# A hybrid recurrent decoder layer on one core: two more Strassen pairs, four fewer filler blocks, and four smaller edits

## The chip, the cores and the metric

The kernel runs on one core of a Trainium2 chip. The metric is the time of one execution on the device, in microseconds (us). A core has five engines with queues of their own: PE (matrix products), DVE (vector), ACT (activation functions, and copies out of the accumulators), POOL (a second, slower vector engine) and SP, which here issues the DMA transfers. PEld is PE's loading of weights. Each engine takes its instructions in the order in which they were written into its queue, and waits on semaphores for the others.

## The reference

One step of a one-layer decoder: 16 meta tokens and 1024 prompt tokens (1040 in one sequence), and 8 samples of 4 tokens; 1072 tokens in all, width 1024, in float32. What comes out for the meta tokens is dropped from the output; their effect on the recurrent states stays.

```
xn = rmsnorm(h) * norm_w
(gq, gk, gv, glr, gg, hq, hf, hi, hg_g, mq, mk, mv, mi, mf, mo, mg, ca, cb, cg, mgate) = split(xn @ w_in)
A (GLA):    S_t = diag(exp g_t) S_{t-1} + k_t^T v_t ; o_t = q_t S_t,     zA = head_rmsnorm(o) * silu(gg)
B (HGRN2):  the same recurrence with f from hf, k = 1 - f, q = silu(hq), zB = head_rmsnorm(o) * silu(hg_g)
C (mLSTM):  stabilised matrix memory,                                    zC = head_layernorm(h * sigmoid(mo)) * silu(mg)
D (conv):   u = ca * sigmoid(cb); yc = causal depthwise conv of width 31, zD = silu(layernorm(yc)) * silu(cg)
mixed = sum_b sigmoid(mgate_b) * (z_b @ w_branch_b)        # four gates of 1024 columns: 32 blocks of 128
y = rmsnorm(h + mixed @ w_out) * final_norm                # and the final states of A, B, C and D
```

## The kernel before

All projections take x transposed, 128 rows by 1072 tokens for each of 8 row blocks. To keep float32 accuracy, each operand is split into a high and a low part (`xh`, `xl` for x; `wh`, `wl` for weights, by `split_w`: ACT makes the high part, POOL or DVE subtracts to get the low one, L138 and L139), and each product is three matmuls: high by high, high by low, low by high (L185 to L187, or L277 to L279).

The program has five stages.

- **Front** (L147 to L181): nine row tiles `h` of x are loaded, normalised (squares on ACT L164, scaling on DVE L167) and transposed by PE in three groups (L174); ACT and DVE then write `xh` (L178) and `xl` (L179) out of the accumulators, of which five are used for this. Beside that, the first gate block's weights `w0` are loaded and split, the split's second half on DVE. `gate_direct(j)` projects one gate block of 128 columns directly: three groups of 352 tokens (the meta tokens are skipped), each of 8 row blocks and 3 products, and writes the sigmoid to memory (`gscr`). Blocks 0 to 3 are done this way, with the small projections between.
- **Pairs**: `pair` computes two blocks of 128 columns at once by Strassen's scheme: x is halved by rows (4 and 4 row blocks) and by tokens (536 and 536), and 7 products replace 8. Each product is done for two halves of 268 tokens, so a pair is 7 x 2 x 4 x 3 = 168 matmuls. Sums of weights are made on DVE (`ta`, `tb`) and split there; sums of results are made on DVE out of the accumulators. Accumulators of tag "a" (`sa`) number two, those of tag "r" (`sb`, `sc`, `sd`) five, in rotation. c11 is what takes the first result out of `sa`, c12, c22 and c21 take the others. `pair_to` uses a pair for gates, for `cg` and for the output gates of the branches, 15 in all; `conv_pair` uses four for `cb` and `ca`. Its results go into a tile `u`, of which there is one; the 31 taps of the convolution are then 31 operations on DVE over 1024 tokens (L386 and L388), which the scheduler puts between the other work at a lower priority.
- **Mixers**: four HGRN units (`hg_unit`), two GLA units for two heads each (`gla_unit`), four mLSTM units. An HGRN or GLA unit goes through seven levels of block sizes 1 to 64 (`levels`): small products `lv` on PE, then DVE scales q and k (L649 to L652) for the next level. In between stand projections of the next unit, and **fillers**: `filler()` takes the next gate block of a list and projects it directly. `linear_unit` calls it `3 - nh` times, which is twice in an HGRN unit (nh = 1) and once in a GLA unit (nh = 2); an mLSTM unit calls it once, the last three times: 16 in all. Of 32 gate blocks 4 are direct in front, 10 in pairs, 2 late and 16 fillers.
- **Branches and output**: the four branch products, gated and added, then the output projection and the final norm.

In a GLA unit the diagonal of the attention is summed apart: `prod` (q times k) is multiplied with two columns of ones (L760), with 128 rows of `prod` at a time as weights. `split3` (L557, accumulator `v9p`) splits the samples' values; its accumulator comes from the pool of projections (three buffers, tag "acc").

The order on each engine is made by a scheduler from its own estimate of durations and from priorities; a change of one piece rearranges the rest.

Of the kernel before, what the change touches and what calls it, by code (L numbers as in the profile page):

```python
# [16 lines left out]
AF = mybir.ActivationFunctionType  # L17
ALU = mybir.AluOpType
# [9 lines left out]
P = 128  # L28
# [37 lines left out]
def trunk(ctx, tc, hx, w_in, w_sm, w_br, w_out, pk, wgk2, mlb, fnorm, s_gla, s_hg, s_c, s_n, s_m, s_cv,  # L66
# [80 lines left out]
    xh = xp.tile([P, KD, NT], F32R, name="xh", tag="xh")  # L147
    xl = xp.tile([P, KD, NT], F32R, name="xl", tag="xl")
    with tc.tile_pool(name="x0", bufs=9, side="right", reuse_waits="tile") as x0:
        hs = []  # L150

        def load_h(i):
            n = min(P, NT - i * P)
            h = x0.tile([P, D], F32, name="h", tag="h")
            DMA.dma_start(h[:n], hx[i * P:i * P + n, :])
            hs.append((h, n))

        for i0 in (0, 3, 6):
            for i in range(i0, i0 + 3):
                load_h(i)  # L160
                h, n = hs[i]
                ss = x0.tile([P, 1], F32, name="ss", tag="ss", bufs=9)
                sq = x0.tile([P, D], F32, name="sq", tag="sq", bufs=1)
                S.activation(sq[:n], h[:n], AF.Square, accum_out=ss[:n])  # L164
                V.tensor_scalar(ss[:n], ss[:n], 1.0 / D, EPS, ALU.mult, ALU.add)
                rs = rsqrt(ss[:n])
                V.tensor_scalar(h[:n], h[:n], rs, None, ALU.mult)  # L167
            if i0 == 0:
                raw0 = load_raw(w_in, OFF["gate"])
            for k in range(KD):  # L170
                ps = mmt("xt")
                t = 0
                for h, n in hs[i0:i0 + 3]:
                    T.transpose(ps[:, t:t + n], h[:n, k * P:(k + 1) * P], ident[:n, :n])  # L174
                    t += n
                nw = col("norm_w", k)
                hi = xh[:, k, i0 * P:i0 * P + t]
                S.activation(hi, ps[:, :t], AF.Identity, scale=nw)  # L178
                V.scalar_tensor_tensor(xl[:, k, i0 * P:i0 * P + t], ps[:, :t], nw, hi, ALU.mult, ALU.subtract)  # L179
            if i0 == 0:  # L180
                w0 = split_w(raw0, E=V)  # L181

    def mm3(ps, wh, wl, ah, al, kd, order=None):
        for i, k in enumerate(order or range(kd)):
# [20 lines left out]
    def gtl(tag, shape, bufs=1, name=None, dt=F32):  # L205
        return pools["gph"].tile(shape, dt, name=name or tag, tag=tag, bufs=bufs)
# [42 lines left out]
        xs.update(a11=a(0, 0), a12=a(KH, 0), a22=a(KH, HT), s1=a(0, HT), s2=(sh[:, 0], sl[:, 0]),  # L249
                  s3=(sh[:, 1], sl[:, 1]), s4=(sh[:, 2], sl[:, 2]))  # L250

    def pair(c0, c1, c11, c12, c22, c21):


        wp = pools["gph"]
# [14 lines left out]
        ps = lambda tag: [pools["ps"].tile([P, 512], F32, name="s" + tag, tag="a" if tag == "a" else "r",  # L270
                                           bufs=2 if tag == "a" else 5)[:, :HS] for _ in range(2)]

        def prod(w, o, x, s, out, start, stop):
            xa, xb = (t[:, :, s * HS:(s + 1) * HS] for t in xs[x])
            for k in range(KH):
                wh, wl = w[0][:, o + k], w[1][:, o + k]
                T.matmul(out, wh, xa[:, k], start=start and k == 0, stop=False, skip_group_check=True)  # L277
                T.matmul(out, wh, xb[:, k], start=False, stop=False, skip_group_check=True)  # L278
                T.matmul(out, wl, xa[:, k], start=False, stop=stop and k == KH - 1, skip_group_check=True)  # L279
# [12 lines left out]
            prod(w2, 0, "s1", s, c[s], True, True)  # L292
            S.activation(h(p5, s), c[s], AF.Copy)
        for s in range(2):
            prod(w1, KH, "a12", s, a[s], False, True)
            c11(s, a[s])
        d = ps("d")
        for s in range(2):
# [3 lines left out]
        V.tensor_tensor(u3, u3, u2, ALU.add)  # L302
        c22(u3)
        for s in range(2):
            prod(w4, 0, "s4", s, c[s], False, True)
            V.tensor_tensor(h(p1, s), h(u2, s), c[s], ALU.add)
        c12(p1)
        for s in range(2):
# [4 lines left out]
    def pair_to(sec, i, dst, func, times=False, base=0):  # L313
# [24 lines left out]
                    DMA.dma_start(dst[j, :, 0:HT - NM], t[:, NM:])  # L338
            return ev

        pair(o, o + P, c11, rest(i + 1, False), rest(i + 1, True), rest(i, True))

    def conv_pair(i):
        u = gtl("u", [P, UW + NSEQ * 34])
        us = u[:, UW:].rearrange("p (s x) -> p s x", x=34)
        G.memset(u[:, 0:30], 0.0)

        def c11(s, ps):
            S.activation(u[:, 30 + s * HS:30 + (s + 1) * HS], ps, AF.Sigmoid)  # L349

        def c12(t):
            V.tensor_tensor(u[:, 30:30 + HT], t, u[:, 30:30 + HT], ALU.mult)

        held = []

        def c21(t):
            S.activation(t, t, AF.Sigmoid)
            m = NP - HT
            V.tensor_tensor(u[:, 30 + HT:UW], held[0][:, :m], t[:, :m], ALU.mult)
            x3 = lambda v: v[:, m:].rearrange("p (s j) -> p s j", j=NDEC)  # L360
            V.tensor_tensor(us[:, :, 30:34], x3(held[0]), x3(t), ALU.mult)

        pair(OFF["cb"] + i * P, OFF["ca"] + i * P, c11, c12, held.append, c21)
        return u, us
# [73 lines left out]
                DMA.dma_start(fscr[p, :, t0:t0 + n], gx)  # L438

    open_pool("gph", bufs=1)  # L440
    gate_direct(0, w=w0)
    gate_direct(1)
    small()
    for j in range(2, NDIR):
        gate_direct(j)
# [2 lines left out]
    open_pool("ps", bufs=2, space=PSUM)  # L448
    open_pool("pm", bufs=1, space=PSUM)
    LATE = (8, 9)  # L450
    NFILL = 16
    fill = list(range(32 - NFILL, 32))
    todo = [("gate", i, gscr, AF.Sigmoid) for i in range(NDIR, 32 - NFILL, 2) if i not in LATE]
    todo += [("cg", i, cscr, AF.Copy) for i in (0, 2)]
# [120 lines left out]
    def vtok(sec, i, ones_col=False):  # L575
# [9 lines left out]
        proj(sec, i, GA, ev)  # L585
        vt = tl("vt", [P, 9, 129], 4)
        (to_tok_v(vf, vt) if ones_col else to_tok(vf, vt, True))
        v9 = split3(x9, 1, "v9", 4, acc_tile("v9p"))
        if ones_col:
            G.memset(vt[:, :, 128:129], 1.0)  # L590
        return vt, v9
# [162 lines left out]
    def linear_unit(uid, qv, nh, k, f, prod, vts, s0, epss, finish, pout, sout):  # L754
        rw = P // nh
        if nh == 2:
            ps = mmt("dg")
            for c in range(9):
                n = csz(c)
                T.matmul(ps[:n, 2 * c:2 * c + 2], prod[:, c * P:c * P + n], onesb, start=True, stop=True)  # L760
            dg = tl("dg", [P, 18], 2)
            V.tensor_copy(dg[:, 0:16], ps[:, 0:16])
            V.tensor_copy(dg[:TAIL, 16:18], ps[:TAIL, 16:18])
            dgv = dg.rearrange("p (c a) -> p c a", a=2)
        atts, tot128, tot16, tot4 = levels(qv, nh, k, f)
        for _ in range(3 - nh):
            filler()
        kt = tl("kt", [P, 9, P], 1)
        to_tok(k, kt)
        xk = tl("xk", [P, 3, NT - NP], 1)  # L770
# [576 lines left out]
```

## Time and profile before

| | us |
|---|---|
| median of 3 runs (1597.06 to 1597.72) | 1597.33 |
| the profiled execution | 1597.18 |
| its span, first to last instruction | 1595.4 |
| PE busy (its matmuls' ends are modelled) | 1558.2 |
| DVE busy | 1035.6 |
| ACT busy | 554.0 |
| POOL busy | 470.9 |

Times in the profile count from the start of the span. A stage is placed by its lines: the front ends near 45 us, the pairs run from about 95 to 510, the mixers from there to about 1270 (the last level of the last GLA unit begins near 1001), and branches and output to the end. PEclk is the share of its full clock that PE was granted. A row of the waits names who waited for whom, then us in total, times and the longest. A row of a timeline has its start, its duration, the engine, the line and operation, and in brackets the idle time before it and what ended it.

### The profile page before, as it was taken

What the parts mean: (1) busy time and instruction counts of PE and PEld (TensorE: products, weight loads), DVE (VectorE), ACT (ScalarE), POOL (GpSimd) and SP (SyncE); (2) the same over time, 40 slices, a digit from 0 to 9 for tenths busy, and PEclk for the clock granted to TensorE, in tenths of its full rate; (3) what the DMA queues carried; (4) which work ended last, traced back from release to release, by engine and by line L of the source; (5) the groups of instructions that cost most, each with busy time, mean ns of one, the idle gap of its engine ahead of it and who ended that gap; (6) DMA issues with size and microseconds to landing.
All of it is one profiled execution on the core that took longest, in us unless ns stands there. A gap on an engine that the chain in (4) does not pass through costs nothing.

```text
span 1595.4 us, 30033 instructions
## 1 busy us (share of the span) xinstructions
PE 1558.2 (98%) x12366; PEld 1496.5 (94%) x12366; DVE 1035.6 (65%) x1827; ACT 554.0 (35%) x1095; POOL 470.9 (30%) x418
## 2 busy tenths in 40 slices
PE   7999999899999999999999999999999999999998
PEld 6999999899999899999998998999999999999886
DVE  7959979999996446444544565476665646744533
ACT  6534343243433333323424323323323244422211
POOL 2222322123223232223232323222322313877300
PEclk9999999999999999999999999999999999999999
DMA  5423233231337113131323132144323277676231
GB/s 190 133 80 101 92 91 107 88 108 51 110 100 236 42 48 104 56 100 56 104 60 94 55 97 82 49 148 135 117 72 88 89 248 224 179 236 208 80 111 54
DMA packets 190572, 176.40 MB, mean 111 GB/s; under 512 B 9260, under 2 KB 164800, under 8 KB 190436
## 3 DMA queue, kind: packets, MB, share of 16 engines
q1 hardware_dynamic: 190436, 174.49, 35.6%
q8 instruction: 97, 1.59, 0.4%
q14 instruction: 39, 0.32, 0.1%
HBM read 122.45 MB, written 52.00 MB: 109 GB/s over the span
## 4 chain that ended last, share of the span: by engine, by line
PE 78%; DVE 16%; issue 3%; DMA 2%; ACT 1%; SPq 0%; DVEq 0%; POOLq 0%; ACTq 0%
PE acc L187 18%; PE acc L185 18%; PE acc L186 18%; DVE y L388 7%; PE lv L636 2%; DVE wl L139 2%; PE sa L277 1%; PE sa L278 1%; PE sa L279 1%; PE sc L278 1%; PE sc L277 1%; PE sc L279 1%; PE sd L279 1%; PE op L800 1%; PE sd L278 1%
## 5 line engine op out<-in xcount | busy, mean ns | idle before, releaser
L139 POOL TENSOR_TENSOR wl<-wraw,wh 128x1024 fp32r<-128x1024 f32 (+1 forms) x124 | 272.2, 2196 | 632.7 <-ACT wh L138 628.0
L185 PE MATMUL acc<-xh,wh 128*128 128x352 f32 (+2 forms) x1320 | 437.5, 332 | 2.1 <-ACT vt L539 1.2
L187 PE MATMUL acc<-xh,wl 128*128 128x352 f32 (+2 forms) x1320 | 436.7, 331 | 0.0
L186 PE MATMUL acc<-xl,wh 128*128 128x352 f32 (+2 forms) x1320 | 435.5, 330 | 0.0
L185 PEld LDWEIGHTS acc<-xh,wh 128*128 128x128 f32 x1320 | 251.7, 191 | 5.6 <-ACT vt L539 1.9
L187 PEld LDWEIGHTS acc<-xh,wl 128*128 128x128 f32 x1320 | 251.0, 190 | 3.2 <-issue 0.9
L186 PEld LDWEIGHTS acc<-xl,wh 128*128 128x128 f32 x1320 | 251.4, 190 | 1.8 <-issue 0.7
L388 DVE SCALAR_TENSOR_TENSOR y<-u,pkt,y 128x1024 f32<-128x1024 f32 x120 | 191.2, 1593 | 0.7
L138 ACT ACTIVATE wh<-wraw 128x512 fp32r<-128x512 f32 (+1 forms) x125 | 110.4, 883 | 231.0 <-PE acc L186 135.8
L185 PE MATMUL acc<-zh,wh 128*128 128x352 f32 x384 | 124.5, 324 | 0.0
L186 PE MATMUL acc<-zl,wh 128*128 128x352 f32 x384 | 124.3, 324 | 0.0
L187 PE MATMUL acc<-zh,wl 128*128 128x352 f32 x384 | 124.2, 324 | 0.0
L277 PE MATMUL sa<-xh,wh 128*128 128x268 f32 x304 | 88.7, 292 | 6.6 <-ACT u L349 6.3
L278 PE MATMUL sa<-xl,wh 128*128 128x268 f32 x304 | 88.2, 290 | 0.0
L279 PE MATMUL sa<-xh,wl 128*128 128x268 f32 x304 | 87.8, 290 | 0.0
L651 DVE TENSOR_TENSOR q<-q,tot 128x256 f32<-128x256 f32 (+3 forms) x96 | 46.4, 483 | 54.5 <-PE lv L636 53.7
L1179 POOL TENSOR_TENSOR mix<-mix,gt 128x352 f32<-128x352 f32 x72 | 73.1, 1030 | 28.9 <-DVE gt L1178 25.7
L185 PEld LDWEIGHTS acc<-zh,wh 128*128 128x128 f32 x384 | 72.2, 188 | 0.4 <-DVE gt L1178 0.4
L187 PEld LDWEIGHTS acc<-zh,wl 128*128 128x128 f32 x384 | 72.3, 188 | 0.0
L186 PEld LDWEIGHTS acc<-zl,wh 128*128 128x128 f32 x384 | 72.2, 188 | 0.0
L277 PEld LDWEIGHTS sa<-xh,wh 128*128 128x128 f32 x304 | 58.3, 192 | 7.3 <-ACT u L349 6.8
L1178 DVE TENSOR_TENSOR gt<-acc,gt 128x352 f32<-128x352 f32 x72 | 36.2, 518 | 39.5 <-PE acc L187 36.6
(393 smaller groups left out, 3367.3 us busy)
## 6 DMA issues: line engine op xcount, KB each, us to landing
wraw<-w_in SPq DMA_DIRECT2D x92, 512.0 KB, 3.9
gt<-gscr SPq DMA_DIRECT2D x30, 528.0 KB, 4.7
gscr<-gd SPq DMA_DIRECT2D x60, 176.0 KB, 1.8
zr<-zscr SPq DMA_DIRECT2D x16, 528.0 KB
wraw<-w_br SPq DMA_DIRECT2D x32, 256.0 KB, 2.9
gt<-sscr SPq DMA_DIRECT2D x12, 528.0 KB, 4.1
zscr<-gt SPq DMA_DIRECT2D x12, 528.0 KB, 2.6
sscr<-u SPq DMA_DIRECT2D x16, 268.0 KB, 2.3
```

What stands on the lines that cost most here:

```text
L138: S.activation(hi[:, :kd], raw[:, :kd], AF.Copy)
L139: (E or G).tensor_tensor(lo[:, :kd], raw[:, :kd], hi[:, :kd], ALU.subtract)
L185: T.matmul(ps, wh(k), ah(k), start=(i == 0), stop=False)
L186: T.matmul(ps, wh(k), al(k), start=False, stop=False)
L187: T.matmul(ps, wl(k), ah(k), start=False, stop=(i == kd - 1))
L277: T.matmul(out, wh, xa[:, k], start=start and k == 0, stop=False, skip_group_check=True)
L278: T.matmul(out, wh, xb[:, k], start=False, stop=False, skip_group_check=True)
L279: T.matmul(out, wl, xa[:, k], start=False, stop=stop and k == KH - 1, skip_group_check=True)
L388: V.scalar_tensor_tensor(ymain, u[:, NM + j:NM + j + NPR], w(j), ymain, ALU.mult, ALU.add)
L651: V.tensor_tensor(qx[:, :, 1], qx[:, :, 1], pv[r, :, 0:1].broadcast_to([rw, nb, h]), ALU.mult)
L1178: V.tensor_tensor(gt[:, t0:t0 + n], ps[:, :n], gt[:, t0:t0 + n], ALU.mult)
L1179: G.tensor_tensor(mixed[j][:, t0:t0 + n], mixed[j][:, t0:t0 + n], gt[:, t0:t0 + n], ALU.add)
```

## The change

- `NFILL` goes from 16 to 12: four gate blocks move from the mixers into two more pairs, at the end of the gates in the list of pairs. `linear_unit` calls one filler whatever nh.
- `prod` in `pair` gets `m`: in `pair_to`, the products a12 and s4 leave out the first 16 tokens (the meta tokens, which nobody reads there) of their first half.
- `conv_pair` writes its sigmoid into a buffer `g11` of its own (the pairs' own tag, two buffers), not into `u`.
- The diagonal sums are made in bands of 32 rows of weights.
- In front, the weights of gate blocks 0 and 1 are both loaded before the later rows of x, and both split with DVE.
- `v9p` takes its accumulator from the general pool (three buffers, tag "mm").

Lines after the convolution's pair move by four, in the units by six: L352 becomes L356, L388 becomes L392, L649 and L651 become L653 and L655, L760 becomes L766.

```diff
-                raw0 = load_raw(w_in, OFF["gate"])
+                raws = [load_raw(w_in, OFF["gate"] + j * P) for j in range(2)]
             for k in range(KD):
...
-            if i0 == 0:
-                w0 = split_w(raw0, E=V)
+                if i0 == 0 and k in (1, 5):
+                    wg01.append(split_w(raws[k // 4], E=V))
...
-    def pair(c0, c1, c11, c12, c22, c21):
+    def pair(c0, c1, c11, c12, c22, c21, m=0):
...
-        def prod(w, o, x, s, out, start, stop):
-            xa, xb = (t[:, :, s * HS:(s + 1) * HS] for t in xs[x])
+        def prod(w, o, x, s, out, start, stop, m=0):
+            m = m if s == 0 else 0
+            out = out[:, m:]
+            xa, xb = (t[:, :, s * HS + m:(s + 1) * HS] for t in xs[x])
...
-            prod(w1, KH, "a12", s, a[s], False, True)
+            prod(w1, KH, "a12", s, a[s], False, True, m)
...
-            prod(w4, 0, "s4", s, c[s], False, True)
+            prod(w4, 0, "s4", s, c[s], False, True, m)
...
-        pair(o, o + P, c11, rest(i + 1, False), rest(i + 1, True), rest(i, True))
+        pair(o, o + P, c11, rest(i + 1, False), rest(i + 1, True), rest(i, True), NM)
...
         u = gtl("u", [P, UW + NSEQ * 34])
+        g11 = stt("g11")
...
-            S.activation(u[:, 30 + s * HS:30 + (s + 1) * HS], ps, AF.Sigmoid)
+            S.activation(g11[:, s * HS:(s + 1) * HS], ps, AF.Sigmoid)
...
-            V.tensor_tensor(u[:, 30:30 + HT], t, u[:, 30:30 + HT], ALU.mult)
+            V.tensor_tensor(u[:, 30:30 + HT], t, g11, ALU.mult)
...
-    gate_direct(0, w=w0)
-    gate_direct(1)
+    for j in range(2):
+        gate_direct(j, w=wg01[j])
...
-    NFILL = 16
+    NFILL = 12
...
-        v9 = split3(x9, 1, "v9", 4, acc_tile("v9p"))
+        v9 = split3(x9, 1, "v9", 4, mmt("v9p"))
...
-                T.matmul(ps[:n, 2 * c:2 * c + 2], prod[:, c * P:c * P + n], onesb, start=True, stop=True)
+                for b in range(0, n, 32):
+                    e = min(b + 32, n)
+                    T.matmul(ps[b:e, 2 * c:2 * c + 2], prod[:, c * P + b:c * P + e], onesb, start=True, stop=True,
+                             skip_group_check=True)
...
-        for _ in range(3 - nh):
-            filler()
+        filler()
```

How the instructions move shows at three places. The first is ACT's order in an HGRN unit, from the unit's values (`vt`) over its levels (`att`) to the level's end (`kt`); `gd` is a filler's eviction, `f` the next unit's forget gate. Before:

```order
L560 ACTIVATE v_7680<-v9p 96x128
L217 ACTIVATE gd<-acc 128x352 x2
L138 ACTIVATE wh<-wraw 128x1024
L217 ACTIVATE gd<-acc 128x352
L688 ACTIVATE att_5615<-own 32x8x32 x4
L217 ACTIVATE gd<-acc 128x352
L676 ACTIVATE att_5615<-lv 32x4x32 x4
L217 ACTIVATE gd<-acc 128x352
L676 ACTIVATE att_5615<-lv 64x4x64 x2
L138 ACTIVATE wh<-wraw 128x1024
L217 ACTIVATE gd<-acc 128x352
L539 ACTIVATE kt<-tt 128x512 x2
```

and with the change:

```order
L217 ACTIVATE gd<-acc 128x352 x2
L138 ACTIVATE wh<-wraw 128x1024
L217 ACTIVATE gd<-acc 128x352
L692 ACTIVATE att_6079<-own 32x8x32 x4
L879 ACTIVATE f<-acc 128x358
L880 ACTIVATE k<-acc 128x358
L680 ACTIVATE att_6079<-lv 32x4x32 x4
L879 ACTIVATE f<-acc 128x358
L880 ACTIVATE k<-acc 128x358
L680 ACTIVATE att_6079<-lv 64x4x64 x2
L138 ACTIVATE wh<-wraw 128x1024
L879 ACTIVATE f<-acc 128x356
```

Where the second filler stood, the next unit's projection hf stands now; before, it came after the levels.

The second place is DVE's order at the third convolution pair, with the last taps into `y`, and `u`, `p`, `sc` of this pair and the next. Before:

```order
L267 TENSOR_TENSOR tb<-wraw,ta 128x512
L139 TENSOR_TENSOR wl<-ta,wh 128x1024
L388 SCALAR_TENSOR_TENSOR y<-u,pkt,y 128x1024 x2
L359 TENSOR_TENSOR u<-u_2958,u_2904 128x504
L361 TENSOR_TENSOR u<-u_2958,u_2904 128x8x4
L352 TENSOR_TENSOR u<-p_2903,u 128x536
```

and with the change:

```order
L139 TENSOR_TENSOR wl<-ta,wh 128x1024
L392 SCALAR_TENSOR_TENSOR y<-u,pkt,y 128x1024
L356 TENSOR_TENSOR u<-p_2909,g_2875 128x536
L363 TENSOR_TENSOR u<-u_2964,u_2910 128x504
L365 TENSOR_TENSOR u<-u_2964,u_2910 128x8x4
L304 TENSOR_TENSOR u_3191<-u_3191,p_3190 128x536
```

The multiplication into `u` stays behind the last tap; its second operand is now `g`.

The third is ACT's order in front, where the first group's `xh` ends and the second's begins. Before:

```order
L178 ACTIVATE xh<-xt,pkt 128x384
L164 ACTIVATE sq,ss<-h 128x1024
L138 ACTIVATE wh<-wraw 128x1024
L164 ACTIVATE sq,ss<-h 48x1024
L178 ACTIVATE xh<-xt,pkt 128x384 x5
L217 ACT_TABLE_LOAD
L217 ACTIVATE gd<-acc 128x352
L178 ACTIVATE xh<-xt,pkt 128x384 x3
```

and with the change:

```order
L178 ACTIVATE xh<-xt,pkt 128x384
L164 ACTIVATE sq,ss<-h 128x1024 x2
L164 ACTIVATE sq,ss<-h 48x1024
L217 ACT_TABLE_LOAD
L217 ACTIVATE gd<-acc 128x352
L178 ACTIVATE xh<-xt,pkt 128x384 x8
```

The table load and the first eviction of a gate now stand ahead of the second group's `xh`, and the split of the second block has gone from here.

More of the change, by code (lines that the diff above doesn't have):

```diff
@@ L149, in trunk @@
     with tc.tile_pool(name="x0", bufs=9, side="right", reuse_waits="tile") as x0:
-        hs = []
+        hs, wg01 = [], []
         def load_h(i):
```

## The prediction

> **What bounds the kernel now.** I read the page first: its totals, and the chain that ended last.
>
> ```profile
> span 1595.4 us, 30033 instructions
> PE 1558.2 (98%) x12366; PEld 1496.5 (94%) x12366; DVE 1035.6 (65%) x1827; ACT 554.0 (35%) x1095; POOL 470.9 (30%) x418
> PE 78%; DVE 16%; issue 3%; DMA 2%; ACT 1%; SPq 0%; DVEq 0%; POOLq 0%; ACTq 0%
> ```
>
> A matmul's end is modelled, so 98% alone proves little. The view of busy time by stretch says more, because its counts give a rate (columns: length, then busy time and count of PE, its weight loads, DVE, ACT and POOL, the granted clock, DMA).
>
> ```profile
> 24.00:31.00 7.00, 5.94 (x24) 5.50 (x24) 7.00 (x15) 3.71 (x6) 1.06 (x2) 0.52 0.37 104
> 125.00:150.00 25.00, 25.00 (x204) 25.00 (x204) 24.16 (x24) 9.06 (x17) 6.91 (x3) 1.00 0.34 100
> 225.00:250.00 25.00, 25.00 (x204) 24.98 (x204) 24.75 (x27) 10.57 (x21) 4.42 (x2) 1.00 0.33 96
> 250.00:275.00 25.00, 25.00 (x204) 25.00 (x203) 24.96 (x26) 8.19 (x14) 7.50 (x3) 1.00 0.29 87
> 275.00:300.00 25.00, 19.18 (x143) 18.18 (x142) 24.79 (x25) 6.37 (x11) 5.86 (x5) 0.94 0.19 54
> 300.00:325.00 25.00, 25.00 (x191) 24.98 (x190) 21.16 (x31) 8.57 (x18) 2.90 (x3) 0.92 0.36 112
> 520.00:565.00 45.00, 42.81 (x582) 40.67 (x581) 20.37 (x45) 17.23 (x30) 9.80 (x8) 0.96 0.18 52
> 825.00:900.00 75.00, 72.70 (x760) 69.28 (x760) 46.01 (x93) 26.78 (x50) 26.25 (x36) 0.95 0.27 79
> 900.00:1000.00 100.00, 96.95 (x956) 91.30 (x956) 53.09 (x131) 28.88 (x67) 27.95 (x36) 0.97 0.25 77
> 1420.00:1440.00 20.00, 20.00 (x127) 20.00 (x126) 6.81 (x12) 3.59 (x5) 14.65 (x16) 1.00 0.65 206
> ```
>
> In the stage of pairs every full stretch holds the same 204 matmuls of 268 columns. About two of them are under way at the edges, so one takes 25/202 = 0.124 us. The last row is a stretch of branch products with 352 columns: 20/125 = 0.160 us. PE runs at these two rates nearly everywhere, so work taken from PE is time taken from the kernel. The exceptions are few: the stretch 275 to 300 (143 matmuls for 204), the front (clock 0.52), and three stretches of the mixers with a clock of 0.95 to 0.97. Then I read PE's waits:
>
> ```profile
> PE sa L277 <- ACT u L349: 6.3, 2, 4.8
> PE lv L636 <- DVE k L652: 4.8, 3, 1.9
> PE tta L538 <- ACT vf L581: 2.3, 1, 2.3
> PE xt L174 <- DVE xl L179: 2.2, 1, 2.2
> PE acc L185 <- ACT vt L539: 1.2, 4, 0.3
> ```
>
> Apart from the first transposes these are nearly all the waits of any size.
>
> **The change part by part.** Gates: four blocks leave the mixers. A direct block has three column groups, eight row blocks and three products: 72 matmuls of 352 columns. So 4 x 72 = 288 x 0.160 = 46.1 us go. Two pairs come, 168 matmuls each: 336 x 0.124 = 41.7 us. Net **-4.4 us**. The pairs' own work on DVE, POOL and ACT I cost at nothing: the list of pairs grows at its end, where the taps of the convolution run out and DVE has room beside PE:
>
> ```profile
> 450.00:475.00 25.00, 25.00 (x204) 25.00 (x203) 25.00 (x32) 10.23 (x20) 5.53 (x3) 1.00 0.29 87
> 500.00:525.00 25.00, 25.00 (x157) 25.00 (x156) 12.92 (x31) 6.18 (x12) 7.04 (x13) 1.00 0.48 146
> ```
>
> Without that room (the first row has none) a pair would add its DVE work, at most the 12.9 us of the second row.
>
> Meta tokens: in 17 of the 21 pairs (all but the four of the convolution) 24 matmuls have 252 columns instead of 268. From the two rates, a column costs (160 - 124)/(352 - 268) = 0.43 ns, so 16 columns 6.9 ns, and 17 x 24 = 408 of them **-2.8 us**. Below, this is bounded by nothing (if a matmul of 252 columns went no faster than one of 268).
>
> Diagonal sums: 9 matmuls a unit become 34, in bands of 32 rows.
>
> ```profile
> 853.91 2.02 PE L760 MATMUL dg<-onesb,prod 128*128 128x2 f32 x18
> 963.86 2.08 PE L760 MATMUL dg<-onesb,prod 128*128 128x2 f32 x18
> 989.95 0.76 PE L636 MATMUL lv<-q,k 128*32 128x32 f32 x64
> ```
>
> Two records stand for one instruction. Now 18 records take 2.02 and 2.08 us, 0.11 us each for two moving columns: the weight load is what they cost. The level products, the third row, load bands of 32 the same way: 64 records in 0.76 us, 0.012 us each. So 68 x 0.012 = 0.8 us a unit, and both units together 4.1 - 1.6 = **-2.5 us**. The Trainium skill speaks against this: "TensorE: Matmul & The Clock Gate", section "LDWEIGHTS (loading the stationary operand)", has a load take its columns over 1.2 ns, and so a band 27 ns. By it 136 loads would be an estimated 3.6 us, the gain 0.5 us, and the sum 2 us higher. The level products are the nearer row, and they contradict a serial load; I take theirs.
>
> Convolution: its sigmoid gets a buffer of its own, where it was written into u.
>
> ```profile
> 293.80 4.68 DVE L388 SCALAR_TENSOR_TENSOR y<-u,pkt,y 128x1024 f32<-128x1024 f32 x2
> 298.52 0.68 ACT L349 ACTIVATE u<-sa 128x268 f32<-128x268 f32 x2 [5.02 <-DVE y L388]
> 298.97 0.59 PE L277 MATMUL sa<-xh,wh 128*128 128x268 f32 x1 [4.83 <-ACT u L349]
> 299.29 0.71 DVE L352 TENSOR_TENSOR u<-p,u 128x536 f32<-128x536 f32 x1
> ```
>
> The taps of the block before still read u, so the sigmoid waits for the last of them, holds both accumulators of tag "a", and PE's next pair waits for those: 6.3 us in two waits. Behind the longer one PE ran slow: the rows 275 to 325 have 0.94 and 0.92, which is 25 x (0.06 + 0.08) = 3.5 us of clock lost. Both go: **-9.8 us**. What is late next is the multiplication L352, which still needs the taps to have ended; on DVE it stands right after them, as before. Queued behind it are the next pair's sums, which free the accumulators of tag "r". By the rotation of five, the pair after that needs one after 36 of its own matmuls, and the accumulator in question was filled at 120 of 168: 84 matmuls or 10.4 us of cover against a lateness of about 5. Bounds: -9.8, and 0 if DVE's lateness comes back at that place. The buffer is one of two that the pairs' stores also use; a store lands in about 2 us and the buffer comes round after two pairs, 41 us, so that costs nothing.
>
> Front: the second gate block's weights are fetched before the later rows of x, and their split moves from POOL to DVE, ahead of the first xl.
>
> ```profile
> 20.94 2.36 POOL L139 TENSOR_TENSOR wl<-wraw,wh 128x1024 fp32r<-128x1024 f32 x1 [1.43 <-ACT wh L138]
> 20.96 2.62 DVE L420 TENSOR_TENSOR wg<-wgr,wg 16x256 fp32r<-16x256 f32 x1
> 21.76 2.46 ACT L178 ACTIVATE xh<-xt,pkt 128x384 fp32r<-128x384 f32 x5
> 24.24 1.28 ACT L217 ACT_TABLE_LOAD   x1
> 25.06 0.90 PE L174 MATMUL xt<-ident,h 128*128 128x128 f32 x3 [2.23 <-DVE xl L179]
> ```
>
> Now PE stops for 2.2 us at 25 because DVE sits 2.62 us on a tiny subtraction beside POOL's split, and the clock of 0.52 that follows costs 7 x 0.48 = 3.4 us. In the change POOL has no split there. But ACT's table load and the gate's first eviction now stand ahead of the second group's eight L178, which come behind three more squares. So the second group's first xh comes at 21.76 + 1.28 and an eviction of 0.5, near 23.5, and later by what the second block's fetch holds up x; its xl follows, and PE stops for a free transpose buffer about as long as now. I take **+0.5 us**. Bounds: -6.2 (stop, 0.6 us before it, and slow clock all go) and +4 (one more slow stretch).
>
> Mixers: four of 16 gate blocks fewer as cover between the levels of the four HGRN units, 11.5 us each. The level rows of one unit show what cover is needed:
>
> ```profile
> 707.45 0.72 PE L636 MATMUL lv<-q,k 128*32 128x16 f32 x63
> 711.70 0.72 PE L636 MATMUL lv<-q,k 128*32 128x16 f32 x63
> 712.22 0.42 DVE L651 TENSOR_TENSOR q<-q,tot 128x256 f32<-128x256 f32 x1 [2.54 <-PE lv L636]
> ```
>
> A level comes every 4.25 us, and DVE still waited 2.54 us for PE there. The order lists of the change keep 20 to 22 matmuls between levels; the next unit's forget gate fills in where the second gate block stood. So I see no new wait. The v9 transpose leaves the accumulators that the next projection needs, and the four waits for vt in the list above go: **-1.2 us**. Bounds: the three mixer waits (4.8 + 2.3 + 1.2 = 8.3) and the clock lost in the three stretches (1.8 + 3.8 + 3.0 = 8.6) together, -16.9; and above, the cover itself, 46.1.
>
> Sum: -4.4 - 2.8 - 2.5 - 9.8 + 0.5 - 1.2 = -20.2. The profiled execution took 1597.18 us (span 1595.4 and 1.8 around it), 0.15 below the median, so **1577.0 us**.
>
> **The rivals.** *DVE keeps the pairs* (16%). DVE is busy for 24.75, 24.96 and 24.79 of 25 us from 225 to 300: it is as full as PE. Removing PE's wait would then only move it to a split or a sum further on. Against it: DVE has 3.8 us free right after, and the place above has 10.4 us of cover. Then 1577.0 + 9.8 = 1586.8.
>
> *The front and the mixers clear too* (15%). DVE's 2.62 us went with POOL's split; without the split in that place the wg subtraction is short, and if ACT's rows are quick enough PE doesn't stop and keeps its clock (-6.7 against my +0.5); with half of the mixers' -16.9 (7.2 beyond my 1.2) 1563. The Trainium skill, "SBUF — State Buffer", section "Who interferes with whom", has such a pair of operations lock each other out, the loser blocked for the whole instruction. The two rows at 20.9 agree. By it alone the front gains.
>
> *The mixers starve* (9%), the one that ends slower. Place: the four HGRN units. If the chain level, DVE, level and the sums after it set a unit's time, PE idles where the block was: up to 11.5 us a unit, 46.1 in all, 1623.1; half of it 1600. It decides from 20.2/4 = 5.1 us a unit, 32 of the 72 matmuls. For it: such small waits exist today (4.8 us). Against: the 2.54 us that DVE waits, and the filled gaps.
>
> *Little moves* (6%): the pure PE work of -9.7 is eaten by new small waits of the rewritten order, 1590 to 1597.
>
> **How the numbers follow.** My own case has 54%, 1570 to 1583. The range from 1563 to 1589 takes in the second and nearly all of the first rival; what is left out is the starving case and most of the last. About 0.2%, 3.2 us, is what a measurement of this kernel can tell from no change. Faster: 54 + 16 + 15 and about half of the last, 88%; same 4%; slower 8%.
>
> **What would show it.** Right: PE's wait for L349's successor gone and the stretch near 290 at clock 1.00; about 0.8 us for each unit's diagonal sums; about 202 matmuls in 25 us in the two new pairs; gaps of about 4.2 us between levels with no wait of PE over 1 us. Wrong: a new wait of sa, sb or sc on DVE in the stage of pairs (first rival); a clock near 1.00 from 24 to 31 (second); waits of lv or tt on DVE in the HGRN units, and the mixers not 40 us shorter (third).

## The result, and the profile after

The changed kernel takes 1585.9 us in the median of four runs (1585.2 to 1587.5), the kernel before 1597.5 us on the same chip: a ratio of 0.992, with a 95% interval of 0.990 to 0.994. On a second chip it was 1585.2 against 1597.3 us, 0.994 (0.992 to 0.996). So 12 us were won, where the prediction's likeliest case had 20. The profiled execution took 1587.48 us with a span of 1585.5, 9.9 us shorter than before.

First the page of the changed kernel: its totals and the shares of the chain that ended last.

```profile
span 1585.5 us, 30405 instructions
...
PE 1545.8 (97%) x12514; PEld 1481.6 (93%) x12514; DVE 1060.6 (67%) x1856; ACT 558.1 (35%) x1108; POOL 471.2 (30%) x417
...
PE 73%; DVE 18%; DMA 3%; issue 3%; ACT 1%; POOL 0%; SPq 0%; DVEq 0%; POOLq 0%; ACTq 0%
```

PE is still the bound, but in the chain DVE went from 16% to 18%. The view of busy time by stretch tells where (columns as in the prediction):

```profile
24.00:31.00 7.00, 4.39 (x17) 4.01 (x18) 6.54 (x13) 4.45 (x9) 1.58 (x2) 0.64 0.09 30
275.00:300.00 25.00, 25.00 (x205) 25.00 (x205) 24.86 (x26) 6.84 (x13) 7.23 (x4) 1.00 0.20 55
300.00:325.00 25.00, 25.00 (x207) 24.98 (x206) 21.46 (x29) 10.73 (x22) 8.72 (x4) 1.00 0.42 128
325.00:350.00 25.00, 23.64 (x187) 22.78 (x185) 24.96 (x28) 6.30 (x12) 6.21 (x2) 1.00 0.34 103
350.00:375.00 25.00, 24.04 (x191) 23.82 (x192) 24.96 (x29) 6.94 (x14) 6.23 (x2) 1.00 0.33 90
425.00:450.00 25.00, 24.02 (x190) 23.16 (x189) 25.00 (x30) 8.29 (x19) 7.40 (x3) 1.00 0.29 87
640.00:655.00 15.00, 12.22 (x168) 10.67 (x169) 11.20 (x26) 5.33 (x8) 1.67 (x2) 0.77 0.61 191
```

The stop near 290 is gone: 205 matmuls between 275 and 300 instead of 143, at full clock. But from 325 to 450 stretches have come that hold 187 to 191 matmuls where an undisturbed one holds 205 to 207, with DVE busy for all of the 25 us. And at 640 there is a new stretch with a clock of 0.77. PE's waits in the changed kernel agree:

```profile
PE lv L640 <- DVE k L656: 5.8, 6, 1.4
PE v9p L561 <- DVE s L838: 2.8, 1, 2.8
PE sb L280 <- DVE p L309: 2.7, 4, 0.8
PE acc L185 <- ACT xh L178: 2.4, 2, 1.7
PE xt L174 <- DVE xl L179: 2.0, 2, 1.1
...
PE tta L542 <- ACT vf L585: 0.8, 1, 0.8
...
PE sa L280 <- DVE g L326: 0.7, 2, 0.4
```

The wait of `sa` for ACT's write into `u` (6.3 us) and the four for `vt` are gone. In their place stand waits of `sb` and `sa` for DVE's sums, and one of `v9p` for DVE's L838. `lv`, which waited three times before, now waits six times.

To see what went where, I split PE's time by stage in every trace. For each matmul shape, the mean distance from one start to the next, taken where nothing disturbs it, times the number of that shape is the stage's **pure** time; the rest of the stage is **lost** to waits and slow clock. In the pairs, where PE has hardly any other shape, the mean takes in every distance below 140 ns; nine tenths of them lie between 119 and 130 ns, and the few longer ones hold a wait. A stage runs from its first matmul to the next stage's: in the kernel before the pairs run from 90.0 to 500.3 us and the mixers to 1297. The front's pure time is 67.8 to 68.0 us in all, and 7.5 to 7.7 us follow the last matmul. How much of a stage counts as lost depends on where the mean is drawn, in the mixers above all, with their many small products; so compare the rows and not the sizes. All runs of the experiments are in the table, in us of the profiled execution; the last column is how much the run's median lies below that of the kernel before on the same chip.

| kernel | first matmul | front, lost | pairs, pure | pairs, lost | mixers, pure | mixers, lost | branches | span | below before |
|---|---|---|---|---|---|---|---|---|---|
| before | 7.9 | 14.1 | 397.1 | 13.3 | 746.1 | 50.7 | 290.5 | 1595.4 | |
| changed | 8.5 | 15.6 | 435.4 | 9.1 | 697.4 | 52.9 | 291.0 | 1585.5 | 11.7 |
| s4 changed, second chip | 8.1 | 15.4 | 435.4 | 8.8 | 697.1 | 52.4 | 290.5 | 1583.2 | 12.1 |
| s2 gates alone | 8.0 | 13.8 | 438.7 | 15.0 | 699.7 | 48.6 | 290.8 | 1590.3 | 4.2 |
| s3 buffer alone | 8.2 | 14.5 | 397.1 | 6.7 | 746.1 | 49.4 | 292.0 | 1589.5 | 8.6 |
| s5 meta and bands alone | 8.2 | 12.9 | 394.2 | 16.2 | 743.2 | 50.1 | 291.4 | 1591.8 | 4.5 |
| e1 v9p undone | 7.5 | 17.1 | 435.5 | 8.8 | 697.0 | 57.4 | 291.4 | 1590.1 | 10.4 |
| e2 buffer undone | 8.2 | 15.4 | 435.4 | 15.0 | 697.1 | 51.7 | 290.9 | 1589.3 | 6.8 |
| e3 half the taps | 8.4 | 14.2 | 435.3 | 0.1 | 697.3 | 51.7 | 291.9 | 1574.6 | 22.6 |
| e4 front undone | 8.0 | 12.6 | 435.3 | 9.6 | 697.0 | 51.2 | 290.5 | 1579.7 | 15.8 |
| s1 five pairs a convolution | 7.9 | 13.5 | 435.3 | 2.6 | 696.7 | 60.7 | 290.0 | 1582.2 | 13.8 |
| x2 and gates last | 8.0 | 12.8 | 435.3 | 0.8 | 697.3 | 49.6 | 291.4 | 1570.8 | 24.3 |
| x3 and rows first | 8.2 | 12.4 | 435.4 | 0.8 | 696.8 | 50.9 | 291.3 | 1571.4 | 23.5 |
| x4 filler moved | 8.1 | 12.6 | 435.3 | 0.7 | 698.2 | 47.4 | 298.6 | 1576.5 | 17.9 |

By this the change took 10.5 us of pure PE work away (38.3 more in the pairs, 48.7 less in the mixers, 0.1 less in front), and the lost time did not fall at all: 4.2 less in the pairs, 2.2 more in the mixers, 1.5 more in front, 0.5 more in the branches, and the first matmul 0.6 later.

### The profile page after: what moved, and what is told of

Same layout as the page of the kernel before. It is cut to its first block, busy times and chain, and to the rows that moved or that the text cites. A ratio compares the mean times of both kernels' runs of the same rounds, so it can differ in the third digit from the quotient of the medians.

```text
span 1585.5 us, 30405 instructions
## 1 busy us (share of the span) xinstructions
PE 1545.8 (97%) x12514; PEld 1481.6 (93%) x12514; DVE 1060.6 (67%) x1856; ACT 558.1 (35%) x1108; POOL 471.2 (30%) x417
## 4 chain that ended last, share of the span: by engine, by line
PE 73%; DVE 18%; DMA 3%; issue 3%; ACT 1%; POOL 0%; SPq 0%; DVEq 0%; POOLq 0%; ACTq 0%
PE acc L185 16%; PE acc L186 16%; PE acc L187 16%; DVE y L392 6%; PE lv L640 2%; DVE so L576 2%; DVE vt L576 2%; PE sc L280 2%; PE sc L281 1%; PE sc L282 1%; PE sa L281 1%; PE sa L280 1%; PE sa L282 1%; PE sd L281 1%; PE sd L282 1%
## 5 line engine op out<-in xcount | busy, mean ns | idle before, releaser
L139 POOL TENSOR_TENSOR wl<-wraw,wh 128x512 fp32r<-128x512 f32 (+1 forms) x123 | 274.7, 2236 | 642.1 <-ACT wh L138 624.4
L185 PE MATMUL acc<-xh,wh 128*128 128x352 f32 (+2 forms) x1224 | 406.2, 332 | 2.4 <-ACT xh L178 2.4
L186 PE MATMUL acc<-xl,wh 128*128 128x352 f32 (+2 forms) x1224 | 404.3, 330 | 0.0
L187 PE MATMUL acc<-xh,wl 128*128 128x352 f32 (+2 forms) x1224 | 403.7, 330 | 0.0
L185 PEld LDWEIGHTS acc<-xh,wh 128*128 128x128 f32 x1224 | 232.8, 190 | 6.6 <-ACT xh L178 2.9
L187 PEld LDWEIGHTS acc<-xh,wl 128*128 128x128 f32 x1224 | 232.4, 190 | 2.8 <-issue 0.7
L392 DVE SCALAR_TENSOR_TENSOR y<-u,pkt,y 128x1024 f32<-128x1024 f32 x120 | 194.0, 1616 | 0.6
L280 PE MATMUL sa<-xh,wh 128*128 128x268 f32 (+1 forms) x336 | 96.4, 287 | 0.7 <-DVE g L326 0.7
L282 PE MATMUL sa<-xh,wl 128*128 128x268 f32 (+1 forms) x336 | 95.8, 285 | 0.0
L281 PE MATMUL sa<-xl,wh 128*128 128x268 f32 (+1 forms) x336 | 95.7, 285 | 0.0
L655 DVE TENSOR_TENSOR q<-q,tot 128x256 f32<-128x256 f32 (+3 forms) x96 | 48.8, 508 | 48.4 <-PE lv L640 47.7
L281 PEld LDWEIGHTS sa<-xl,wh 128*128 128x128 f32 x336 | 63.3, 188 | 0.0
```

The costliest lines, as they stand in the source:

```text
L139: (E or G).tensor_tensor(lo[:, :kd], raw[:, :kd], hi[:, :kd], ALU.subtract)
L185: T.matmul(ps, wh(k), ah(k), start=(i == 0), stop=False)
L186: T.matmul(ps, wh(k), al(k), start=False, stop=False)
L187: T.matmul(ps, wl(k), ah(k), start=False, stop=(i == kd - 1))
L392: V.scalar_tensor_tensor(ymain, u[:, NM + j:NM + j + NPR], w(j), ymain, ALU.mult, ALU.add)
L655: V.tensor_tensor(qx[:, :, 1], qx[:, :, 1], pv[r, :, 0:1].broadcast_to([rw, nb, h]), ALU.mult)
```

## The experiments

Executions of one kernel differ by some us, and the 95% interval of a ratio is 0.14 to 0.31% to either side (2 to 5 us). So a verdict rests on the median and on the place in the trace together. The unaltered changed kernel ran again beside three of the runs (s1 to s3):

> The changed kernel unaltered, for the comparison on the same chip: 1585 to 1588 us, 0.992 of the kernel before.

It took 1585.2 us, and its stages lose what they lost on the first chip (the table's second and third row).

**What the convolution's buffer is worth.** One run takes it out of the changed kernel:

```diff
-            S.activation(g11[:, s * HS:(s + 1) * HS], ps, AF.Sigmoid)
+            S.activation(u[:, 30 + s * HS:30 + (s + 1) * HS], ps, AF.Sigmoid)
...
-            V.tensor_tensor(u[:, 30:30 + HT], t, g11, ALU.mult)
+            V.tensor_tensor(u[:, 30:30 + HT], t, u[:, 30:30 + HT], ALU.mult)
```

> The changed kernel with the convolution's sigmoid written into u again. Forecast's term: the wait of 6.3 us and 3.5 us of lost clock near 290 come back, 1595.7 us. Theory after the result: DVE sets the pace of the pairs, so the buffer saved only what DVE's lateness did not take back elsewhere (in all some 2 to 3 us): 1588 to 1589, and the small waits of sa, sb and sc on DVE's sums between 320 and 480 grow fewer while the wait on L349's successor is back.

1590.9 us, a ratio of 0.996 (0.995 to 0.998). PE's waits in it:

```profile
PE sa L280 <- ACT u L352: 7.1, 3, 4.8
...
PE sb L280 <- DVE p L309: 2.2, 2, 1.7
```

The old wait is back, and the pairs lose 15.0 us instead of 9.1. From 320 to 480 us, though, it loses 2.8 us where the changed kernel loses 8.6. So the buffer is worth 5.9 us in the changed kernel, neither 9.8 nor the 2 to 3 of my theory after the result. The reverse run puts the buffer alone into the kernel before (the same lines, the other way):

> The kernel before with the convolution's own sigmoid buffer alone. Forecast's term of -9.8: 1587.7. Theory after the result: the wait near 290 and its slow clock go, and DVE's lateness comes back in small waits of sb, sc and sa between 320 and 480: 1592 to 1595.

1588.7 us, 0.995 (0.993 to 0.996). The pairs lose 6.7 us instead of 13.3, 6.5 less before rounding. In the slices of 40 us, the 9.3 us lost from 280 to 320 fell to 0.0 and the 1.8 from 160 to 200 to nothing, and from 320 to 480 the loss rose from 2.2 to 6.7. So 11 us go, and 4.5 come back later in the same stage; within the change, by the run before this one, 5.8 come back of 11.5.

**What sets the pace there.** In the changed kernel half of the taps are left out, which is DVE's work alone:

```diff
-        for j in range(1, 31):
+        for j in range(1, 16):
             V.scalar_tensor_tensor(ymain, u[:, NM + j:NM + j + NPR], w(j), ymain, ALU.mult, ALU.add)
```

> The changed kernel with 15 of the 30 accumulating taps of each convolution left out (60 operations of about 1.6 us on DVE, nothing on PE); it leaves out that part of the convolution. Theory: DVE's taps make the sums of the pairs late, and the waits and slow stretches of PE between 125 and 480 (about 11 us above the pure matmul spacing) mostly go: 1575 to 1579 us. Rival: the waits come from the order of the sums, not from how full DVE is: 1584 to 1587.

1575.1 us, 0.986 (0.983 to 0.989). Its busy time by stretch:

```profile
325.00:350.00 25.00, 25.00 (x205) 25.00 (x205) 22.89 (x28) 8.39 (x15) 4.29 (x3) 1.00 0.38 114
350.00:375.00 25.00, 25.00 (x205) 25.00 (x204) 11.19 (x18) 9.45 (x18) 5.55 (x3) 1.00 0.18 47
...
425.00:450.00 25.00, 25.00 (x205) 25.00 (x205) 19.32 (x31) 11.28 (x21) 3.96 (x2) 1.00 0.45 147
```

DVE has room, and PE holds 205 matmuls in each; the pairs lose 0.1 us, and no wait of PE is left there. So the 9.1 us that the changed kernel loses in the pairs are owed to DVE's taps, practically all of them.

How a tap makes a sum late shows in the changed kernel's timeline of DVE (start, duration, operation):

```profile
338.98 1.22 DVE L139 TENSOR_TENSOR wl<-ta,wh 128x1024 fp32r<-128x1024 f32 x1
340.11 5.65 DVE L392 SCALAR_TENSOR_TENSOR y<-u,pkt,y 128x1024 f32<-128x1024 f32 x2
345.68 0.70 DVE L304 TENSOR_TENSOR u<-u,p 128x536 f32<-128x536 f32 x1
346.31 1.27 DVE L392 SCALAR_TENSOR_TENSOR y<-u,pkt,y 128x1024 f32<-128x1024 f32 x1
347.51 0.42 DVE L309 TENSOR_TENSOR p<-u,sc 128x268 f32<-128x268 f32 x1
```

POOL's row of the same time, with two splits in it:

```profile
338.47 6.21 POOL L139 TENSOR_TENSOR wl<-wraw,wh 128x1024 fp32r<-128x1024 f32 x2 [17.05 <-ACT wh L138]
```

And PE's, with its wait in brackets:

```profile
347.98 0.39 PE L280 MATMUL sb<-sh,wh 128*128 128x268 f32 x1 [0.72 <-DVE p L309]
```

Two taps take 5.65 us while POOL makes two splits; alone a tap takes 1.27. The sum L309 behind them frees `sc`, and PE waits for it with the next pair's `sb`. This is no single case: of the 120 taps in the changed kernel's trace, the 78 that meet no instruction of POOL take 1.29 us at most, and the 42 that do take 2.25 us in the mean and up to 3.44. By these figures POOL costs the taps some 41 us of DVE (42 x 0.98). Whether splits moved away from POOL would free DVE as well as fewer taps do, no run tries.

**The gates alone.** Two more pairs and 12 fillers in the kernel before:

```diff
-    NFILL = 16
+    NFILL = 12
...
-        for _ in range(3 - nh):
-            filler()
+        filler()
```

> The kernel before with the two more pairs and 12 fillers alone. Forecast's term of -4.4: 1593. Theory after the result: the same PE work leaves (46.4 us against 41.7), but with one filler less per HGRN unit PE reaches the second HGRN unit while DVE is still behind (a wait of about 3 us and a slow clock of 3.4): 1597 to 1600. Rival: the mixers starve, over 1600.

1593.1 us, 0.998 (0.997 to 1.000): 4.2 us in the medians, near the forecast's term, with an interval that reaches from under 1 us to 5. The pure times say 41.6 more and 46.4 less, 4.8 in all (forecast 41.7 and 46.1). My theory after the result fell: the mixers do get a new stop in the second HGRN unit, as this run's waits show, but the one in the first unit (the 6.1 us lost from 520 to 560 before) goes, and they lose 48.6 us in place of 50.7. The pairs lose 1.8 more.

```profile
PE lvt L640 <- DVE s L831: 1.6, 1, 1.6
```

**The shorter matmuls and the bands alone.** The parts with `m` and the bands of 32 rows, in the kernel before:

```diff
-            prod(w1, KH, "a12", s, a[s], False, True)
+            prod(w1, KH, "a12", s, a[s], False, True, m)
...
+                for b in range(0, n, 32):
```

> The kernel before with the skipped meta tokens and the diagonal sums in bands alone. Forecast's terms: -2.8 and -2.5, so 1592. Theory after the result: the bands give 2.4; of the 3.2 us of shorter matmuls about half are lost where DVE sets the pace (three of the four stretches with taps): 1593 to 1594. By the Trainium skill's page on TensorE (a serial load of 27 ns a band) the bands would give 0.5: 1594.

1592.5 us, 0.998 (0.996 to 0.999). The pairs' pure time falls by 2.9 us (the forecast's term has 2.8 for 17 pairs; this kernel has 15 of them, for which the same sum gives 2.5), and their lost time rises by 2.9: from the first matmul to the next stage's they last 410.4 us, as before. Alone the meta tokens bring nothing, since DVE doesn't become faster. What they bring in the changed kernel, no run takes apart. The mixers' pure time falls by 2.9. Most of that is the bands; in the changed kernel they take:

```profile
861.28 0.73 PE L766 MATMUL dg<-onesb,prod 128*32 128x2 f32 x68
...
958.25 0.73 PE L766 MATMUL dg<-onesb,prod 128*32 128x2 f32 x68
```

0.73 us a unit against 2.02 and 2.08, so 2.6 us; the forecast had 0.8 a unit. By the Trainium skill ("TensorE: Matmul & The Clock Gate", section "LDWEIGHTS (loading the stationary operand)"), 68 loads of 32 columns would be an estimated 1.8 us; the trace disagrees.

**v9p.** The changed kernel with its accumulator back in the pool of projections:

```diff
-        v9 = split3(x9, 1, "v9", 4, mmt("v9p"))
+        v9 = split3(x9, 1, "v9", 4, acc_tile("v9p"))
```

> The changed kernel with v9p back in an accumulator of the projections (tag acc). Theory: the changed kernel's new wait of v9p in the first HGRN unit (2.8 us) and the slow clock behind it (6.8 us at half, 3.4) come from the tag mm, whose three buffers are held there until a DVE operation of the sums; so both go, up to four waits for vt come back (1.2): 1581 us. Rival: PE's stop there is DVE's lateness and only moves to another tile: 1585 to 1588.

1587.3 us, 0.995 (0.992 to 0.997): not faster. PE's timeline at the stop in the changed kernel:

```profile
641.89 0.33 PE L640 MATMUL lv<-q,k 128*32 128x32 f32 x14
644.99 0.45 PE L561 MATMUL v9p<-ident,x 128*96 128x128 f32 x1 [2.78 <-DVE s L838]
```

And in this run:

```profile
646.00 0.29 PE L644 MATMUL lvt<-q,k 128*48 128x48 f32 x2 [1.63 <-DVE s L838]
```

The stop is the same DVE instruction's lateness, with another tile's name. (It lies in the second HGRN unit, not in the first as the expectation has it: the first unit's `v9p` is at 573.7 us.) DVE's timeline in the changed kernel shows what it is behind, the mLSTM's rows (the operations on 4 partitions):

```profile
641.57 1.07 DVE L937 TENSOR_TENSOR lf<-b,segm 4x896 f32<-4x896 f32 x1
...
642.81 1.21 DVE L943 TENSOR_TENSOR ig<-ct,b 4x1024 f32<-4x1024 f32 x1
...
644.27 1.27 DVE L838 TENSOR_TENSOR s<-s,sds 128x512 f32<-128x512 f32 x2
```

The run's mixers lose 57.4 us; its profiled execution was the slowest of six, so that size is not to be trusted, only that no gain came.

**The front.** The changed kernel with the old front (one block fetched ahead, its split behind the eight `xl`, the second block's split on POOL):

```diff
-                raws = [load_raw(w_in, OFF["gate"] + j * P) for j in range(2)]
+                raw0 = load_raw(w_in, OFF["gate"])
...
-                if i0 == 0 and k in (1, 5):
-                    wg01.append(split_w(raws[k // 4], E=V))
+            if i0 == 0:
+                w0 = split_w(raw0, E=V)
```

> The changed kernel with the front as before (one block's weights fetched ahead, the second block's split on POOL behind the gate). Forecast's term of +0.5 us: 1585.3. Theory after the result: the front cost about 1.9 us (first matmul 0.6 us later, 1.3 us of small waits): 1584. Rival: the front's edit is a gain that other stages hide: 1587 to 1588.

1581.9 us, 0.990 (0.987 to 0.993). The front loses 12.6 us against 15.6 and 15.4, and its first matmul comes at 8.0 against 8.5 and 8.1: about 3 us. Kernels with one and the same front differ too, though: the nine with the old one lose 12.4 to 14.5 us (13.2 in the mean), the five with the new one 14.2 to 17.1 (15.5). So by all runs the new front costs some 2.3 us. The changed kernel's timeline ahead of and at its stop, rows of DVE, ACT and PE:

```profile
21.77 0.41 DVE L424 TENSOR_TENSOR wg<-wgr,wg 16x256 fp32r<-16x256 f32 x1
...
23.18 1.28 ACT L217 ACT_TABLE_LOAD   x1
...
24.84 2.46 ACT L178 ACTIVATE xh<-xt,pkt 128x384 fp32r<-128x384 f32 x5
...
25.47 0.43 PE L185 MATMUL acc<-xh,wh 128*128 128x352 f32 x1 [1.68 <-ACT xh L178]
...
26.38 1.65 DVE L179 SCALAR_TENSOR_TENSOR xl<-xt,pkt,xh 128x384 fp32r<-128x384 f32 x3
...
27.04 0.90 PE L174 MATMUL xt<-ident,h 128*128 128x128 f32 x3 [1.14 <-DVE xl L179]
```

The subtraction L424 is down from 2.62 to 0.41 us without POOL's split, as one rival had it; yet PE stops, for ACT.

**A version with more room for the taps.** From here on the front is the old one. First, four pairs instead of three behind each convolution pair:

```diff
         conv_states(i, *cu)
         pair_to(*todo.pop(0))
+        pair_to(*todo.pop(0))
```

> The changed kernel with the front as before, and with four pairs instead of three behind each convolution pair, so that its taps have five pairs' time instead of four. Theory: a pair takes 20.6 us of PE and about 10.3 us of DVE without taps (12.7 to 13.4 us in 25 at the end of the pairs), and 31 taps about 50 us, which five pairs hold (51 us free) and four do not (41 us); so PE's small waits on DVE's sums between 320 and 480 (about 8 us above the pure spacing) go: 1574 us. Rival: the waits come from the order of taps and sums inside a pair and stay: 1580 to 1583.

1583.5 us, 0.992 (0.990 to 0.995): not faster than the old front alone. The pairs lose 2.6 us instead of 9.6, as the theory had it, and the mixers 60.7 instead of 51.2. The taps now last past the end of the pairs (the last one ends at 535.9 us, PE's last matmul of a pair starts at 527), and PE waits at the seam, as its waits show:

```profile
PE acc L185 <- DVE u L313: 5.1, 1, 5.1
```

So the taps' lateness must have work without DVE behind it. Next, the pairs whose results are multiplied on DVE (gg, hg, mg) come early in the list and the plain gates last:

```diff
+    todo = [ggs[0], gts[0], ggs[1], gts[1], hgs[0], gts[2], hgs[1], mgs[0],
+            mgs[1], cgs[0], cgs[1], mos[0], mos[1]] + gts[3:]
```

> As the run with four pairs behind each convolution pair, and the pairs whose results are multiplied on DVE (gg, hg, mg: 2.9 us more of DVE each) come first, the plain gates last. Theory: DVE has then about 13 us less to do behind the last convolution pair, so its taps end before the pairs do, the wait of 5.1 us at the end of the pairs and the slow clock behind it go, and the stretch from 160 to 560 stays at the pure spacing: 1575 to 1577 us. Rival: the lateness of DVE turns up at another place: 1582 to 1584.

1572.6 us, 0.985 (0.983 to 0.987): 24.3 us below the kernel before, twice what the change won, and the best of all versions here. The run with the old front alone has 15.8 of these; the other 8.5 are won by the room for the taps and the order, and the pairs lose 0.8 us instead of 9.6. Two of its stretches with taps, and the seam:

```profile
350.00:375.00 25.00, 25.00 (x207) 24.98 (x206) 24.93 (x26) 8.89 (x18) 6.80 (x3) 1.00 0.35 105
...
450.00:475.00 25.00, 25.00 (x207) 24.98 (x207) 24.80 (x27) 10.50 (x22) 4.72 (x2) 1.00 0.31 92
525.00:550.00 25.00, 25.00 (x156) 25.00 (x155) 10.35 (x30) 6.42 (x12) 7.46 (x13) 1.00 0.49 150
```

DVE is as full as before, yet PE holds 207: what matters here is not how full DVE is but whether its backlog is gone when the next convolution pair, or the end of the stage, asks for it.

**The stop in the mixers.** Two runs on top of this try to take it away. First the mLSTM's rows ahead of the first HGRN unit:

```diff
-    hg_unit(0)
     ml_n0()
     ct = ml_rows()
+    hg_unit(0)
```

> As x2_gates_last, and the mLSTM's rows (some 14 us of DVE on 4 partitions) ahead of the first HGRN unit instead of behind it. Theory: these rows are what makes DVE late in the second HGRN unit, where PE waits 2.8 us for v9p and is slow behind it; so both go there, 6 us less than x2_gates_last: 1569 to 1571 us. Rival: the rows then make DVE late in the first unit, and nothing is won: within 2 us of x2_gates_last, or slower.

1573.5 us, 0.986 (0.983 to 0.989): the rival. The stop in the second unit is gone, and one in the first unit has come, by PE's waits:

```profile
PE acc L185 <- DVE q L552: 3.3, 1, 3.3
```

Then a filler from the end of the last mLSTM unit to the first HGRN unit:

```diff
-        filler()
+        for _ in range(2 if len(fill) == 12 else 1):
+            filler()
...
-        for _ in range(3 if h == 3 else 1):
+        for _ in range(2 if h == 3 else 1):
```

> As x2_gates_last, with one of the three fillers of the last mLSTM unit given to the first HGRN unit, which has two again. Theory: the changed kernel's wait of 2.8 us in the second HGRN unit and the slow clock behind it (6.8 us at half) are there because one filler less lets PE come 11.5 us earlier to a place where DVE is still busy with the mLSTM's rows; with the filler back both go, about 6 us: 1567 us. Rival 1: DVE's lateness belongs to the rows' place in its queue, which the scheduler sets anew with the filler, and the wait stays or turns up next to it: 1571 to 1574. Rival 2: the last mLSTM unit needs its third filler as cover: slower than 1574.

1581.0 us, 0.990 (0.988 to 0.991): slower than the version without it, the second rival, though the theory was right at its place. No wait of `v9p` is left, and the mixers lose 47.4 us instead of 49.6; but the branches last 7.2 us longer. Their largest wait in this run is

```profile
PE acc L185 <- DVE mix L1186: 1.5, 2, 1.2
```

It is one of many small ones. Around the start of the branches, 30 us hold 172 matmuls in this run (the first row) and 195 in the version without the move (the second):

```profile
1280.00:1310.00 30.00, 27.50 (x172) 25.90 (x171) 20.59 (x34) 15.04 (x34) 9.62 (x8) 1.00 0.81 245
```

```profile
1270.00:1300.00 30.00, 30.00 (x195) 29.92 (x194) 18.38 (x31) 16.68 (x33) 7.95 (x7) 1.00 0.81 249
```

So the third filler of the last unit had covered the start of the branches; as long as it did, no wait of any size showed it.

## Why the prediction was right, and where it was wrong

Faster was right, and 1585.9 us lies in the range from 1563 to 1589. The time of the likeliest case, 1577, is 8.9 us too low, and the time lies outside that case's own 1570 to 1583; the rival *DVE keeps the pairs* gave 1586.8, and the range held the time because it took that rival in. Its signs, new waits of `sa`, `sb` and `sc` for DVE, came; that its number lies so near is in part luck, since it put all of the miss into the pairs, and half of it lies elsewhere. By the terms:

| term | forecast | measured in the traces |
|---|---|---|
| gates | -4.4 | -4.8 (gates alone, pure) |
| meta tokens | -2.8 | -2.9 pure alone (15 pairs), and +2.9 lost again |
| diagonal bands | -2.5 | -2.6 |
| convolution | -9.8 | -6.5 alone, -5.9 within the change |
| front | +0.5 | +2.1 against before, +2.3 in the mean of all runs |
| mixers, v9p | -1.2 | +2.2 (mixers, lost) |
| branches | none | +0.5 |

The three terms of pure PE work held: their sum was -9.7, and 10.5 us went. A matmul of 268 columns has a mean distance of 123.8 ns before and 123.7 in the changed kernel, one of 252 columns 116.4, so a skipped column is worth 0.46 ns where the forecast had 0.43. The rest is lost time. The span fell by 9.9 us where the forecast had 20.2, and the 10.3 us between them are 3.9 in the convolution's term, 3.4 in the mixers, 1.7 from the other edits in the pairs, 1.6 in front and 0.5 in the branches, less the 0.8 of pure work.

The step that failed is in the convolution's part: "By the rotation of five ... 10.4 us of cover against a lateness of about 5". At the place it spoke of, it was right, and the wait with its slow clock went as priced (11 us with the one near 194). But the cover was counted for one accumulator, once. A backlog of DVE isn't paid off at one place: with PE no longer held back, DVE stayed behind, and 4.5 us (s3) or 5.8 (e2 against the changed kernel) came back 30 to 190 us later, in waits of `sb`, `sa`, `sc` and `sd` for DVE's sums. The rival named this, priced it with all of 9.8 and got 16%; the rows that spoke for it (DVE busy for 24.75 to 24.96 of 25 us) stood in the same fence as those from which the term took its slow clock. Nearly half of it was true by itself (s3). More came with the other edits: more pairs and shorter matmuls ask more of a DVE that is already the slower one. With the old buffer these add 1.8 and 2.9 us to the pairs' lost time (s2, s5). The parts do not quite add up: 13.3 + 1.8 + 2.9 - 6.5 = 11.5, and 9.1 was measured; which of them loses less beside the others, no run shows. So the term of the meta tokens was right in size, but it should not simply have been summed: by itself, in a stage where DVE sets the pace, PE's shorter work won no time.

In the mixers the forecast's "I see no new wait" failed: `lv` waits six times (longest 1.4 us), and `v9p` once for 2.8 us, with 3.4 us of clock lost behind it (15 x 0.23 in the stretch from 640). The edit of `v9p` isn't its cause (e1): the stop of the first HGRN unit moved to the second (s2). What the four filler blocks covered was small; the rival *the mixers starve* didn't come about, as the mixers' lost time in s2 is 2.1 us less than before. Between s2 and the changed kernel it rises by 4.3 us, and which edit does that, no run shows.

In front the sign was right and the reason too (ACT's table load and eviction stand ahead of the second group's `xh`), but the time was not: I put the first `xh` near 23.5, and it came at 24.84, because the table load ahead of it began at 23.18, behind the squares, and not at 21.76. The rival in which the front clears fell, although its own observation (the short subtraction) came true: the clock from 24 to 31 was 0.64, where it asked for one near 1.00.

## What to carry to other kernels

When two engines are both full in a stage, a wait that is taken from one place can be owed again later, here about half of it: count the second engine's backlog up to the point where something needs it gone (the next reuse of its buffer, the end of the stage), not the cover at the place of the wait. Terms that shorten the other engine's work should not simply be added there; here giving DVE's work room (x2) won 8.5 us more than the old front alone, beside the 11.7 us of all six edits together. And cover that is taken from one end of a stage should be looked for at the other: a filler that shows no wait may be what prevents one.

## What the hardware showed that I had not expected

A tap on DVE takes 1.27 us, and two take 5.65 us beside two splits on POOL (6.21 us): more than twice as long, though the two engines work on different tiles there. The Trainium skill, "SBUF — State Buffer", section "Who interferes with whom", says that a DVE instruction with two inputs from SBUF contends with a POOL instruction that reads SBUF; the rows agree, and the prediction used this for one subtraction in front without looking at the 120 taps.

An operation on 4 partitions costs DVE as much as one on 128: L943 with 4x1024 elements takes 1.21 us, the same operation with 128x1024 (L139 at 338.98) 1.22. The mLSTM's rows, tiny as their data are, hold DVE long enough to stop PE.

A wait of PE of 2.78 us, behind some 4 us of small matmuls with gaps, was enough for a slow clock. PE's timeline in the changed kernel, 5 and 6 us behind that wait:

```profile
649.97 0.49 PE L187 MATMUL acc<-xh,wl 128*128 128x352 f32 x1
650.26 0.49 PE L185 MATMUL acc<-xh,wh 128*128 128x352 f32 x1
650.56 0.37 PE L186 MATMUL acc<-xl,wh 128*128 128x352 f32 x1
650.77 0.32 PE L187 MATMUL acc<-xh,wl 128*128 128x352 f32 x1
650.93 0.32 PE L185 MATMUL acc<-xh,wh 128*128 128x352 f32 x1
```

Up to 650.56 the matmuls start 0.29 to 0.30 us apart, from 650.77 on 0.16.
